# A two-layer block on one core: idle products at the opening, longer planner allowances, and modulations moved to other places

## The chip, the cores and the metric

The kernel runs on one core of one Trainium2 chip. The metric is the device time of one execution in microseconds. The kernel before took 1059.36 us as the median of three runs (1059.28 to 1059.82). The engines are named TensorE (PE in profile rows), VectorE (DVE), ScalarE (ACT), GpSimd (POOL) and SyncE (SP); SyncE's queue issues the transfers of the weights.

## The reference

Everything is fp32, for a batch of one, 512 tokens, width 1024. A first layer (a mixture of a pooling branch and of forgetting attention) feeds a second one whose norms and residuals are modulated by a vector c.

```
layer 1:  h = rmsnorm(concat(16 meta tokens, x)) * norm_g
  u, zp, q, k, v, za, f, gp, ga = split(h @ w_in)
  yp = pool(u) * silu(zp)        # 4 groups of 128 channels: trailing means over 2, 4, 8, 16, minus u
  ya = attention(q, k, v, decay from f) * silu(za)                  # 8 heads of 64
  h  = h0 + (sigmoid(gp) * (yp @ w_up_pool) + sigmoid(ga) * (ya @ w_up_attn)) @ w_out
  x  = rmsnorm(h) * final_norm_g, without the meta tokens
layer 2:  sh1, sc1, gt1, sh2, sc2, gt2 = split(silu(c) @ w_ada + b_ada)     # six modulations
  h  = rmsnorm(x) * (1 + sc1) + sh1;  q, k, v of 16 heads = h @ w_in_2
  o  = 8 stick-breaking heads, 8 heads of attention in chunks (band and bias, q and k normalised)
  x  = x + gt1 * (o @ w_o)
  h  = rmsnorm(x) * (1 + sc2) + sh2
  x  = x + gt2 * (relu(h @ w1)^2 @ w2)                              # 1024 -> 4096 -> 1024
```

## The kernel before, in words

Each fp32 operand of a large product is split into a high and a low part, and each product is done as three: high by high, high by low, low by high (`mm3`, L149). A weight arrives by one transfer into a raw tile `wr` (a ring of five), ScalarE casts it to the high part `wh`, and GpSimd or VectorE subtracts to get the low part `wl` (L128, both rings of four). Results stand in eight PSUM banks.

The stages, in the time of the profiled execution: first norm and values to about 62 us, attention and dense products of layer one to 222, the up products to 372, `w_out` and the joint norm (the final norm of layer one, and the first norm of layer two) to 424, the values and the first strip's queries and keys to 446, attention and dense products of layer two with the first rows of `w_o` to 672, the remaining rows and the second norm to 692, then the product with `w1` in a form with fewer multiplications (lines L1204 to L1206 and L1276 to L1304 write the hidden rows `hid`), from 870 on the product with `w2`.

TensorE's order is written out by the program; those of the other engines are set by a scheduler at build time. Where attention and dense products lie side by side, a planner (`weave`, L73) takes turns: each stream yields the cost of a step in ns of a planned clock, or a name to wait for, and a step that needs a result of another engine is held until an allowance (the `LAT_` constants, in planned ns) has passed since the step that makes it. The allowances are thus only numbers that set TensorE's order; nothing waits for them on the chip. In `attn2` (L1012) a unit is one strip of 128 queries of one head: `scores` (products, then softmax on the other engines), and two units later its `turn`, which transposes the weights (L1002); after eight units `pv2` multiplies by the values. `dense2` gives the queries and keys of the next pairs, of which the last four are normalised first (L861 to L885; L878 and L879 are products with the squares), and then the first rows of `w_o`.

A modulation is computed on VectorE: `ada(v, j)` (L203) loads 512 KB of `w_ada` and adds two of eight blocks of rows into an accumulator (L215 the first, L217 each other, 128x512); four steps make a half of one of the six vectors, which TensorE then sums over partitions (L234). The list `todo` holds the steps, `ada_step` takes the next, and they are sprinkled over other work. The vector 5 is the gate of the last residual.

The opening: x and `norm_g` are loaded (L292, L293), `norm_g` is spread over the partitions by TensorE (L360), VectorE normalises the first rows (L329), TensorE transposes them (L333), and ScalarE and VectorE split them (L334, L335). In the pooling branch `u_tile(g)` (L543) makes g + 1 adds of a tile with itself shifted (L555), and L558 subtracts u.

## Time and profile before

| | |
|---|---|
| median of the runs | 1059.36 us |
| profiled execution | 1057.35 us, span 1055.2 us |
| mean granted clock of TensorE | 0.994 |
| busy: TensorE, VectorE, ScalarE, GpSimd | 1012.8, 628.3, 561.8, 301.0 us |
| read from HBM | 119.82 MB, 118 GB/s over the span |

The span runs from the first to the last instruction of one execution. A row of the timeline gives start and duration, engine, line, operation, names (out<-in), tile and, in brackets, how long the engine had been idle before it and what ended that. A group of equal instructions that follow one another is one row with a count. The granted clock is a share of full speed: 1.00 is 2.4 GHz, 0.50 is 1.2 GHz.

### The profile page before, as it was taken

How to read it: one execution, taken by the hardware profiler on the slowest of the kernel's cores; microseconds unless marked ns; L12 is line 12 of the kernel's file. 1: busy time of each engine (PE TensorE's matmuls, PEld its weight loads, DVE VectorE, ACT ScalarE, POOL GpSimd, SP SyncE). 2: the span in 40 equal slices, each digit the busy share in tenths (PEclk: the TensorE clock that was granted, in tenths of full speed). 3: DMA queues.
4: the chain of work that ended last, by engine and by line, in shares of the span. 5: the costliest groups of instructions: out<-in, count | busy, mean ns of one | idle time of the engine just before them, and what ended most of it. 6: DMA issues, size and time to landing. Idle time of an engine off the chain costs nothing.

```text
span 1055.2 us, 15524 instructions
## 1 busy us (share of the span) xinstructions
PE 1012.8 (96%) x5918; PEld 857.8 (81%) x5918; DVE 628.3 (60%) x1184; ACT 561.8 (53%) x1082; POOL 301.0 (29%) x157
## 2 busy tenths in 40 slices
PE   7999999899999999999899988999999979999998
PEld 5987977768888888987678866799999978888886
DVE  6465866764533669367777476569588862611115
ACT  6365654454545645466687686347567753222220
POOL 3322123423322543203202115122121233233330
PEclk9999999999999999999999999999999999999999
DMA  8442533454543566326421234443234334633302
GB/s 238 126 122 63 154 94 102 138 138 122 149 112 100 181 198 192 128 72 189 126 63 61 68 101 140 146 113 82 66 94 120 121 120 135 177 109 100 100 20 80
DMA packets 136059, 125.54 MB, mean 119 GB/s; under 512 B 8141, under 2 KB 112417, under 8 KB 135986
## 3 DMA queue, kind: packets, MB, share of 16 engines
q1 hardware_dynamic: 135986, 124.56, 40.6%
q8 instruction: 46, 0.75, 0.3%
q14 instruction: 27, 0.22, 0.1%
HBM read 119.82 MB, written 4.73 MB: 118 GB/s over the span
## 4 chain that ended last, share of the span: by engine, by line
PE 76%; DVE 9%; issue 5%; ACT 3%; DMA 3%; POOL 3%; SPq 0%; DVEq 0%; POOLq 0%; ACTq 0%
PE ps L150 19%; PE ps L152 18%; PE ps L151 18%; PE ps L1204 4%; PE ps L1206 3%; PE ps L1205 3%; DVE ada L217 2%; PE ps L963 2%; DMA wr<-in_w_ada_dram 2%; POOL wl L128 1%; DMA wr<-in_w_in_dram 1%; PE ps L519 1%; PE ps L438 1%; PE ps L439 1%; DVE QK L427 1%
## 5 line engine op out<-in xcount | busy, mean ns | idle before, releaser
L128 POOL TENSOR_TENSOR wl<-wr,wh 128x1024 fp32r<-128x1024 f32 x99 | 248.1, 2511 | 577.7 <-ACT wh L131 567.1
L131 ACT CAST wh<-wr 128x1024 fp32r<-128x1024 f32 x130 | 136.3, 1050 | 106.5 <-PE ps L151 55.7
L150 PE MATMUL ps<-hh,wh 128*128 128x512 f32 (+1 forms) x352 | 129.7, 368 | 0.0
L151 PE MATMUL ps<-hl,wh 128*128 128x512 f32 (+1 forms) x352 | 125.1, 355 | 0.0
L152 PE MATMUL ps<-hh,wl 128*128 128x512 f32 (+1 forms) x352 | 124.8, 355 | 0.0
L150 PE MATMUL ps<-wh,T 128*128 128x512 f32 x256 | 101.0, 394 | 0.0
L152 PE MATMUL ps<-wh,T 128*128 128x512 f32 x256 | 100.4, 392 | 0.0
L151 PE MATMUL ps<-wl,T 128*128 128x512 f32 x256 | 100.2, 391 | 0.0
L217 DVE SCALAR_TENSOR_TENSOR ada<-wr,vc,ada 128x512 f32<-128x512 f32 x84 | 81.7, 972 | 11.4 <-DMA wr<-in_w_ada_dram 10.4
L150 PEld LDWEIGHTS ps<-hh,wh 128*128 128x128 f32 x352 | 66.3, 188 | 20.4 <-issue 11.5
L152 PEld LDWEIGHTS ps<-hh,wl 128*128 128x128 f32 x352 | 66.4, 189 | 9.7
L151 PEld LDWEIGHTS ps<-hl,wh 128*128 128x128 f32 x352 | 66.4, 189 | 7.7
L128 DVE TENSOR_TENSOR wl<-wr,wh 128x1024 fp32r<-128x1024 f32 x31 | 41.4, 1336 | 29.1 <-ACT wh L131 29.1
L152 PEld LDWEIGHTS ps<-wh,T 128*128 128x128 f32 x256 | 48.1, 188 | 11.4
L151 PEld LDWEIGHTS ps<-wl,T 128*128 128x128 f32 x256 | 48.1, 188 | 10.7
L150 PEld LDWEIGHTS ps<-wh,T 128*128 128x128 f32 x256 | 48.1, 188 | 10.6
L150 PE MATMUL ps<-h2h,wh 128*128 128x512 f32 (+1 forms) x144 | 54.9, 381 | 0.0
L1206 PE MATMUL ps<-QK,wl 128*128 128x256 f32 x192 | 53.7, 280 | 0.0
L1204 PE MATMUL ps<-QK,wh 128*128 128x256 f32 x192 | 53.7, 279 | 0.0
L1205 PE MATMUL ps<-PT,wh 128*128 128x256 f32 x192 | 53.4, 278 | 0.0
L152 PE MATMUL ps<-h2h,wl 128*128 128x512 f32 (+1 forms) x144 | 53.3, 370 | 0.0
L151 PE MATMUL ps<-h2l,wh 128*128 128x512 f32 (+1 forms) x144 | 53.1, 369 | 0.0
(412 smaller groups left out, 2672.6 us busy)
## 6 DMA issues: line engine op xcount, KB each, us to landing
wr<-in_w_in_dram SPq DMA_DIRECT2D x64, 512.0 KB, 5.8
wr<-in_w_dram SPq DMA_DIRECT2D x64, 512.0 KB, 4.1
wr<-in_w_ada_dram SPq DMA_DIRECT2D x48, 512.0 KB, 4.9
wr<-in_w_out_dram SPq DMA_DIRECT2D x12, 512.0 KB, 3.5
wr<-in_w_o_dram SPq DMA_DIRECT2D x12, 512.0 KB
xr<-in_x_dram SPq DMA_DIRECT2D x8, 512.0 KB
wr<-in_w_up_pool_dram SPq DMA_DIRECT2D x8, 256.0 KB
wr<-in_w_up_attn_dram SPq DMA_DIRECT2D x8, 256.0 KB, 3.3
```

The source lines that it names most:

```text
L128: (eng or pool).tensor_tensor(dst, raw, f(hi), op=OP.subtract)
L131: act.copy(dst_hi, raw)
L150: pe.matmul(ps, lh, rh, start=start, stop=False)
L151: pe.matmul(ps, lh, rl, start=False, stop=False)
L152: pe.matmul(ps, ll, rh, start=False, stop=stop)
L217: dve.scalar_tensor_tensor(acc, raw[:, q, :], cs, acc, op0=OP.mult, op1=OP.add)
L427: dve.scalar_tensor_tensor(A[e][other], src[own], scale, f(A[e][own]), op0=OP.mult, op1=OP.subtract)
L438: pe.matmul(ps, A[e][:, sa], B[e][:, sb], start=True, stop=False)
L963: pe.matmul(ps[:, d0:], ntri if j2 == j else nones, part[:, SOFF[j2]:SOFF[j2] + 512 - d0], start=False, stop=part is sl and j2 == j, skip_ ...
L1204: pe.matmul(ps, wh, bh, start=first and k == 0, stop=False, **go)
L1205: pe.matmul(ps, wh, bl, start=False, stop=False, **go)
L1206: pe.matmul(ps, wl, bh, start=False, stop=k == 3, **go)
```

## The change

`norm_g` is loaded ahead of x. Sixteen products of a constant tile with itself (`warm`, results unused) are written into TensorE's order at the opening: six at the very start, four after the spreading of `norm_g`, six ahead of the first weights product. In the last pooling group the adds are done by VectorE. Several allowances are longer, and that of a chunked unit depends on its strip. Modulation 4, which opened the list of layer two (its steps lay in the joint norm and the attention), is computed in layer one, beside the up products, three steps and not two in each of the last four of these; `ada_all()` after `weave` in layer one becomes an assertion that nothing is left. Two of the values' chunks in `v2_chunk` share banks in pairs. The steps of modulation 5 begin with a copy of a column of `hid[31]` into the accumulator, so that the accumulation stands behind the last hidden row. The diff:

```diff
@@ -34,14 +34,16 @@
 ORDER = (0, 1, 4, 2, 5, 3, 6, 7)
 LAST_SB = 3
 DENSE = (1, "v2", 4, 2, 5, 3, "v3", 6, 7)
-LAT_CA = 5600.0
+LAT_CA = 6000.0
 LAT_SM = 3200.0
 LAT_SB = 4000.0
-LAT_CM = 3200.0
+LAT_CM = (3200.0, 3800.0, 4400.0, 5000.0)
 LAT_QK = 2600.0
-LAT_SQ = 3800.0
-LAT_ADA = 4000.0
+LAT_SQ = 5000.0
+LAT_ADA = 6500.0
 LAT_PV = 600.0
+LAT_PV2 = 1500.0
+LAT_QK2 = 3800.0
 
 
 def f(ap):
@@ -146,10 +148,10 @@
         split(hi, lo, raw, eng or (dve if lo_turn[0] % dve_turn[0] == 0 else pool))
         return hi, lo
 
-    def mm3(ps, lh, ll, rh, rl, start, stop):
-        pe.matmul(ps, lh, rh, start=start, stop=False)
-        pe.matmul(ps, lh, rl, start=False, stop=False)
-        pe.matmul(ps, ll, rh, start=False, stop=stop)
+    def mm3(ps, lh, ll, rh, rl, start, stop, **go):
+        pe.matmul(ps, lh, rh, start=start, stop=False, **go)
+        pe.matmul(ps, lh, rl, start=False, stop=False, **go)
+        pe.matmul(ps, ll, rh, start=False, stop=stop, **go)
 
     def rstd(r, ss, n):
         parts = ss.shape[0]
@@ -200,7 +202,7 @@
 
     ada_acc = {}
 
-    def ada(v, j):
+    def ada(v, j, late=None):
         half, k = j // 4, 2 * (j % 4)
         raw = wts.tile([128, 2, 512], F32, name="wr", tag="wr", bufs=5)
         x = a["w_ada_2"]
@@ -208,6 +210,8 @@
                                   ap=[[6 * D, 128], [128 * 6 * D, 2], [1, 512]]))
         if k == 0:
             ada_acc[0] = consts.tile([128, 512], F32, name="ada", tag="ada", bufs=1)
+            if late is not None:
+                dve.tensor_copy(ada_acc[0][:, :1], late)
         acc = ada_acc[0]
         for q in range(2):
             cs = vc[:, V_C + k + q:V_C + k + q + 1]
@@ -289,8 +293,16 @@
 
     x_meta = wt([128, D], "PT")[:NM]
     gn = wt([1, D], "QK")
+    sp.dma_start(gn, rows(a["norm_g"], 0, 1, D, 0, D))
     sp.dma_start(xr[0], rows(a["x"], 0, 128, D, 0, D))
-    sp.dma_start(gn, rows(a["norm_g"], 0, 1, D, 0, D))
+    idle = bank()
+
+    def warm(n):
+
+        for _ in range(n):
+            pe.matmul(idle[:, :128], ones_f, ones_f, start=True, stop=True)
+
+    warm(6)
 
     wv = {}
 
@@ -358,9 +370,11 @@
     gnb = [bank(), bank()]
     for b in range(2):
         pe.matmul(gnb[b], ones_f[:1], gn[:, 512 * b:512 * b + 512], start=True, stop=True)
+    warm(4)
     load_wv(0)
     sp.dma_start(xr[1], rows(a["x"], 128, 128, D, 0, D))
     first_norm(xr[0], 128, NM, *x0)
+    warm(6)
     vt = [v_tile(t) for t in range(5)]
     next(vt[0])
     x1 = x_stats(xr[1], 128)
@@ -552,7 +566,7 @@
         prev, w = u, 1
         for q in range(g + 1):
             s = wt([128, NP], "T")
-            pool.tensor_tensor(s[:, 2 * w - 1:], prev[:, 2 * w - 1:], prev[:, w - 1:NP - w], op=OP.add)
+            (dve if g == 3 else pool).tensor_tensor(s[:, 2 * w - 1:], prev[:, 2 * w - 1:], prev[:, w - 1:NP - w], op=OP.add)
             prev, w = s, 2 * w
         pf = prev[:, NM:]
         dve.scalar_tensor_tensor(pf, pf, 1.0 / w, u[:, NM:], op0=OP.mult, op1=OP.subtract)
@@ -621,9 +635,9 @@
             ada_step()
         for m in range(8):
             yield from ups(m)
-            ada_step(2)
-
-    todo += [(v, k) for v in (0, 1, 3) for k in range(8)]
+            ada_step(2 if m < 4 else 3)
+
+    todo += [(v, k) for v in (0, 1, 3, 4) for k in range(8)]
     UT = wt([128, NP], "T")
     pool.memset(UT, 1.0)
     pool.affine_select(UT, UT, pattern=[[1, NP]], base=0, channel_multiplier=-1, compare_op=OP.is_ge, fill=0.0)
@@ -652,7 +666,7 @@
         act.copy(Cm[0:8, c0:c0 + n], src[:8, :n])
         dve.tensor_tensor(Cm[32:40, c0:c0 + n], src[:8, :n], f(Cm[0:8, c0:c0 + n]), op=OP.subtract)
     weave((SHARE1, attn1()), (1.0, dense1()))
-    ada_all()
+    assert not todo
 
     def col_norm(tts, t, hh_, hl_, gcol, bcol):
         for b in range(4):
@@ -805,7 +819,7 @@
         act.copy(V2[t][:, 256 * c:256 * c + 256], ps[:, :256])
 
     def v2_chunk(c):
-        pss = [bank() for _ in range(4)]
+        pss = [b[:, 256 * q:256 * q + 256] for b in (bank(), bank()) for q in range(2)]
         base = (1024, 1280, 2560, 2816)[c]
         for kk in range(2):
             wh, wl = weights([wcols(w_in2, 3 * D, base, 256, 4, 512 * kk)], [4, 256])
@@ -813,10 +827,11 @@
                 for q in range(4):
                     k = 4 * kk + q
                     h, l = h_of(k, 128 * t, 128)
-                    mm3(pss[t][:, :256], h, l, wh[:, q, :], wl[:, q, :], k == 0, k == KT - 1)
+                    mm3(pss[t], h, l, wh[:, q, :], wl[:, q, :], k == 0 and t % 2 == 0, k == KT - 1,
+                        skip_group_check=True)
                     yield 325
                 if kk:
-                    act.copy(V2[t][:, 256 * c:256 * c + 256], pss[t][:, :256])
+                    act.copy(V2[t][:, 256 * c:256 * c + 256], pss[t])
 
     vw = [v2_weights(0), v2_weights(1)]
     w_in2_0 = [weights([wcols(w_in2, 3 * D, c0, 128)], [KT, 128]) for c0 in (0, 512)]
@@ -859,7 +874,7 @@
         else:
             yield from gate(w_in2_tile(128 * p, q_out), p)
             yield from w_in2_tile(512 + 128 * p, k_out)
-        mark(("qk2", p))
+        mark(("qk2", p), LAT_QK2)
 
     def gate(gen, p):
 
@@ -1027,7 +1042,7 @@
                     yield ("qk2", u[0])
                 yield kind[0](*u)
                 ada_step()
-                ripe[n] = clk[0] + (LAT_SB if kind is sb else LAT_CM)
+                ripe[n] = clk[0] + (LAT_SB if kind is sb else LAT_CM[u[1]])
                 if n % 8 == 7:
                     mark(("att", u[0]), 800.0)
             if 0 <= n - LAG < len(units):
@@ -1036,7 +1051,7 @@
             m = n - LAG - 1
             if m >= 0 and m % 8 == 7:
                 p = units[m][1]
-                yield at(clk[0] + LAT_PV)
+                yield at(clk[0] + LAT_PV2)
                 yield from pv2(p, [st[p, e][2] for e in range(2)])
                 if p == LAST_SB:
                     MX[1] = wt([128, 4, 512], "Y")
@@ -1080,7 +1095,7 @@
             rows_mm(pss_o, hts[0], rows_weights(a["w_o_2"], k, kept2, ["Y", "Y", "Y", "PT"]), k, x_of, k == 0, k == KT - 1)
             yield 2560
 
-    todo += [(v, k) for v in (4, 2) for k in range(8)]
+    todo += [(v, k) for v in (2,) for k in range(8)]
     run(qk2_sb(0))
     for c in range(2):
         for t in range(2, 4):
@@ -1370,15 +1385,15 @@
     for ft in range(32):
         if ft:
             w2_operands()
+        hs, ws = held[ft]
         if 2 <= ft < 10:
-            ada(5, ft - 2)
+            ada(5, ft - 2, hid[31][:, :1])
             if ft % 4 == 1:
                 ada_due.pop()
                 gate_sum(ft // 4 - 1)
         if ft == 10:
             load_gt(5, hid[31])
             gt = gtp[5]
-        hs, ws = held[ft]
         if ft < 32 - LAST:
             for t in range(4):
                 for n in range(2):
```

Three places of the orders are shown; the changed file's lines have numbers 2 to 15 higher than those of before.

VectorE at the last pooling group, before. L483 to L490 are the softmax of a strip of the first attention, L507 and L505 copies of its transposed weights, L558 the end of the pooling group:

```order
L483 ISA T,nmx<-ps,strip,nmx 128x264
L483 ISA nmx 128x1
L489 RECIPROCAL sums<-sums 128x1
L490 TENSOR_SCALAR T<-T,sums 128x528
L507 COPY PT<-ps 128x3x128
L558 SCALAR_TENSOR_TENSOR T<-T 128x512
L128 TENSOR_TENSOR xp<-T,xp 128x512
L505 COPY PTm<-ps 16x128 x2
```

and the same place now, where L569 is the shifted add:

```order
L497 ISA T,nmx<-ps,strip,nmx 128x264
L497 ISA nmx 128x1
L569 TENSOR_TENSOR T<-T 128x527
L569 TENSOR_TENSOR T<-T 128x525
L503 RECIPROCAL sums<-sums 128x1
L569 TENSOR_TENSOR T<-T 128x521
L504 TENSOR_SCALAR T<-T,sums 128x528
L569 TENSOR_TENSOR T<-T 128x513
L521 COPY PT<-ps 128x3x128
L572 SCALAR_TENSOR_TENSOR T<-T 128x512
L519 COPY PTm<-ps 16x128
L130 TENSOR_TENSOR xp<-T,xp 128x512
```

The four adds, which stood on GpSimd, are now spread over VectorE's softmax instructions, three of them ahead of the second normalise (L490, now L504).

VectorE in the second joint norm, before; L217 is a step of a modulation, the rest belongs to the norm:

```order
L723 TENSOR_TENSOR xr<-ps,xr 128x512
L728 TENSOR_TENSOR jn_3780<-jn_3780,jn_3781 128x1
L217 SCALAR_TENSOR_TENSOR ada<-wr,vc,ada 128x512
L160 TENSOR_SCALAR rs_t<-rs_y,rs_m 128x1
L217 SCALAR_TENSOR_TENSOR ada<-wr,vc,ada 128x512
L161 SCALAR_TENSOR_TENSOR jr_3782<-rs_t,rs_y 128x1
L725 TENSOR_TENSOR xr<-xr,V 128x512
L730 TENSOR_SCALAR jn_3780<-jn_3780,jr_3782 128x1
L727 TENSOR_TENSOR jn_3817<-jn_3817,jn_3818 128x1
L217 SCALAR_TENSOR_TENSOR ada<-wr,vc,ada 128x512
```

and now:

```order
L737 TENSOR_TENSOR xr<-ps,xr 128x512
L742 TENSOR_TENSOR jn_3838<-jn_3838,jn_3839 128x1
L162 TENSOR_SCALAR rs_t<-rs_y,rs_m 128x1
L163 SCALAR_TENSOR_TENSOR jr_3840<-rs_t,rs_y 128x1
L744 TENSOR_SCALAR jn_3838<-jn_3838,jr_3840 128x1
L739 TENSOR_TENSOR xr<-xr,V 128x512
L159 TENSOR_SCALAR rs_m<-jn_3838 128x1
```

The modulation's steps are gone from between the norm's instructions.

TensorE at the end of layer-two attention, before. L1002 transposes a unit's weights, L150 to L152 with `mxs` are dense products of `w_o`'s first rows, each block four by three of them (the left-out lines repeat them):

```order
L1002 MATMUL ps<-ident,T 128x128 x2
L150 MATMUL ps<-Y,mxs 128x512
...
L152 MATMUL ps<-Y,mxs 128x512
L1002 MATMUL ps<-ident,T 128x128 x3
L150 MATMUL ps<-Y,mxs 128x512
L151 MATMUL ps<-PT,mxs 128x512
...
L151 MATMUL ps<-PT,mxs 128x512
L152 MATMUL ps<-Y,mxs 128x512
L1002 MATMUL ps<-ident,T 128x128 x4
```

and now, where L452 and L453 are the last units' scores, L1017 the transposes and L931 the products with the values:

```order
L452 MATMUL ps<-QK 128x384
L453 MATMUL ps<-lz_606,QK 128x384
L1017 MATMUL ps<-ident,T 128x128
L452 MATMUL ps<-QK 128x512
L453 MATMUL ps<-lz_606,QK 128x512
L1017 MATMUL ps<-ident,T 128x128 x9
L931 MATMUL ps<-PT,V_3933 64x512 x2
L931 MATMUL ps<-PT,V_3934 64x384 x2
L931 MATMUL ps<-PT,V_3935 64x256 x2
```

Before, a block of dense products lay ahead of each of the last two turns; now the last three turns, nine transposes in all, follow the last scores directly.

## Rows read from the trace of the kernel before

**Rows 1.** Page, part 1: busy us (share of the span), instructions.

```profile
PE 1012.8 (96%) x5918; PEld 857.8 (81%) x5918; DVE 628.3 (60%) x1184; ACT 561.8 (53%) x1082; POOL 301.0 (29%) x157
```

**Rows 2.** Waits of TensorE: releaser, us in total, times, longest.

```profile
PE ps L1204 <- DVE hid L1276: 5.4, 1, 5.4
...
PE ps L879 <- DVE PTm L128: 4.6, 4, 1.5
PE ps L1002 <- DVE sums L993: 3.5, 2, 2.3
PE ps L519 <- ACT PT L504: 3.1, 1, 3.1
PE ps L333 <- DVE PT L329: 3.1, 2, 1.8
PE ps L664 <- DVE PTm L733: 2.6, 1, 2.6
PE ps L1002 <- ACT T L992: 2.1, 2, 1.6
PE ps L878 <- ACT PTm L131: 1.9, 3, 1.0
```

**Rows 3.** Stretches: length, busy us (instructions) by engine, granted clock, DMA share, GB/s.

```profile
445.70:622.00 176.30, 167.00 (x970) 135.00 (x969) 122.52 (x251) 123.46 (x264) 34.06 (x27) 1.00 0.33 96
622.00:692.00 70.00, 64.19 (x311) 48.57 (x310) 43.05 (x113) 39.75 (x85) 21.51 (x9) 0.98 0.46 135
864.10:867.50 3.40, 3.22 (x15) 3.22 (x16) 0.46 (x2) 0.88 (x2) 0.00 (x0) 0.50 0.70 228
```

**Rows 4.** Timeline of TensorE at the start: start, duration, instruction, idle before.

```profile
4.63 3.75 PE L360 MATMUL ps<-QK,ones_f 1*128 1x512 f32 x4 [4.63 <-DMA QK<-in_norm_g_dram]
...
12.53 0.41 PE L152 MATMUL ps<-Y,hl 128*128 128x256 f32 x1
12.74 0.41 PE L150 MATMUL ps<-Y,hh 128*128 128x256 f32 x1
...
15.05 0.28 PE L152 MATMUL ps<-Y,hl 128*128 128x256 f32 x1
15.17 0.28 PE L150 MATMUL ps<-Y,hh 128*128 128x256 f32 x1
```

**Rows 5.** Timeline of GpSimd, 200 to 210 us.

```profile
203.75 2.58 POOL L128 TENSOR_TENSOR wl<-wr,wh 128x1024 fp32r<-128x1024 f32 x1
206.30 2.43 POOL L555 TENSOR_TENSOR T<-T 128x521 f32<-128x521 f32 x2
```

**Rows 6.** Timeline of VectorE, 200 to 212 us.

```profile
203.33 0.75 DVE L490 TENSOR_SCALAR T<-T,sums 128x528 f32<-128x528 f32 x1
...
208.76 0.69 DVE L558 SCALAR_TENSOR_TENSOR T<-T 128x512 f32<-128x512 f32 x1 [4.21 <-POOL T L555]
```

**Rows 7.** Timeline of all engines around 166 us.

```profile
165.94 2.38 POOL L128 TENSOR_TENSOR wl<-wr,wh 128x1024 fp32r<-128x1024 f32 x1
...
166.01 2.86 DVE L558 SCALAR_TENSOR_TENSOR T<-T 128x512 f32<-128x512 f32 x1 [0.95 <-POOL T L555]
```

**Rows 8.** Timeline of VectorE in the second joint norm.

```profile
401.82 0.62 DVE L215 TENSOR_SCALAR ada<-wr,vc 128x512 f32<-128x512 f32 x1 [1.93 <-DMA wr<-in_w_ada_dram]
...
422.27 1.00 DVE L733 TENSOR_SCALAR PTm<-xr,jr,jr 128x512 f32<-128x512 f32 x2
```

**Rows 9.** Groups of line L217, 372 to 424 us: count, min/median/max ns, starts.

```profile
L217 DVE SCALAR_TENSOR_TENSOR ada<-wr,vc,ada x7: 740/741/748, 405.9 to 418.9; 128x512 f32<-128x512 f32 x7
```

**Rows 10.** Timeline of TensorE at the end of layer-two attention.

```profile
641.80 0.52 PE L1002 MATMUL ps<-ident,T 128*128 128x128 f32 x3 [2.28 <-DVE sums L993]
```

**Rows 11.** Timeline of VectorE at the last gate's modulation.

```profile
858.74 5.15 DVE L217 SCALAR_TENSOR_TENSOR ada<-wr,vc,ada 128x512 f32<-128x512 f32 x2 [0.76 <-DMA wr<-in_w_ada_dram]
863.82 0.41 DVE L1276 TENSOR_TENSOR hid<-ps,hid 128x256 f32<-128x256 f32 x1
```

**Rows 12.** Page, part 6: loads of w_in's raw tiles, us to landing.

```profile
wr<-in_w_in_dram SPq DMA_DIRECT2D x64, 512.0 KB, 5.8
```

## The prediction

> **What bounds the kernel now.** I began with the busy table of the page: TensorE is busy for 1012.8 of 1055.2 us, 96% of the span, and it does its products one after the other [rows 1]. So the end is set by TensorE's own work, which this change leaves alone but for sixteen small products, and by whatever keeps TensorE idle or slow. Two views name that rest. The table of waits for TensorE lists single places, 1 to 5 us each [rows 2]. The stretches view gives the granted clock: from 864.1 to 867.5 us it was 0.50, the lower level (1.2 GHz), with TensorE busy 3.22 of the 3.40 us [rows 3]. There are four such stretches, each 3.4 us long, and each begins about a microsecond or less after one of the long waits of [rows 2] has ended (L519, L664, the longer L1002 by L993, L1204). Work at half rate takes twice its time, so a stretch costs 3.4 / 2 = 1.7 us: a long wait has its own length as a price and 1.7 us behind it. The opening is a fifth slow stretch: at 12.53 us products of 256 columns start 0.21 us apart, at 15.05 us 0.12 us apart [rows 4].
>
> I sum against the profiled execution, 1057.35 us long (the span of 1055.2 and 2.15 around it). The median of the runs, 1059.36, stands 2.0 above it, and I add that at the end. About 2.1 us (0.2%) is what can be told from no change here.
>
> **Opening.** TensorE waits 4.63 us for norm_g, whose load stood behind x's; the 4 pieces of L360 then take 3.75 us [rows 4]. With the two loads exchanged the pieces start about as much sooner as one issue takes, some 0.4 us, and x lands as much later: nothing net. Of the idle products six fill the wait for norm_g, four the wait for the first normalised rows (part of the 3.1 us at L333, [rows 2]), and six stand straight before the first weights product. Gain: some eleven slow products at 0.21 - 0.12 = 0.09 us, 1.0 us, if the clock is up by then, and 0.7 us since VectorE and ScalarE now do the second half of the norm ahead of a weights split. Cost: a product of 128 idle columns appears in no row. The nearest are L360's, 3.75 / 4 = 0.94 us for 512 columns at the low clock, so 0.24 us for 128. Only the last six stand in front of ready work: 1.4 us at that rate, 0.7 at twice it, which I take. Together +1.0; bounds -1.0 to +2.5 (part of the 3.1 us goes too).
>
> **Last pooling group's adds, from GpSimd to VectorE.** TensorE's L519 waits 3.1 us [rows 2]. GpSimd does a weights split of 2.58 us first and the last two adds of L555 from 206.30 [rows 5], VectorE's L558 comes at 208.76 after 4.21 us idle [rows 6], and ScalarE's copy of PT, which L519 needs, stands behind the cast of that result. The change puts four adds of about 0.7 us each (L558's price, [rows 6]) on VectorE. But in the new order three of them stand before the normalise L490, and GpSimd is free to run its split at that time. What that does is in the rows: the L558 at 166.01 us took 2.86 us where 0.69 is its price alone, and a GpSimd split ran from 165.94 for 2.38 us [rows 6, 7]. So I let one add be held until the split has ended. L490, at 203.33 before [rows 6], comes 3 to 4 us later, and TensorE, which had no wait there, waits about 2.6 us for it: most of the wait is moved, not gone. Gain 3.1 - 2.6 = 0.5, and a half chance of saving the 1.7 us behind it: +1.3. Bounds 0 (all moved) and 3.1 + 1.7 = +4.8 (no add is held).
>
> The Trainium skill, "SBUF — State Buffer", section "Who interferes with whom", speaks against this edit: VectorE shares its second pair of memory ports with GpSimd, and of two instructions that need the pair, a VectorE operation with two inputs in SBUF being one, the later is locked out until the earlier ends. The trace agrees (2.86 against 0.69 us). Without such a rule the pooling term would be its upper bound and the forecast 3.5 us lower.
>
> **One modulation moved to layer one.** In the second joint norm VectorE waits 1.93 us for a w_ada tile, spends 0.62 us on L215 [rows 8], and then 7 times 0.741 us, 5.2 us, on L217 among the norm's own instructions [rows 9]: 7.7 us in all ahead of L733 at 422.27 us [rows 8], for which TensorE's L664 waits 2.6 us [rows 2]. In the new order none of this stands there. L733 then comes up to 7.7 us earlier; it needs only 2.6. So the wait goes (2.6) and its slow stretch (1.7): +4.3. What ends last there afterwards is TensorE. Bounds +2.6 (the stretch stays) and +5 (some tenths of waiting for h2l behind the late L215 go too). The eight steps, 16 operations of 0.74 us and 8 tiles of 512 KB, now lie beside the up products of layer one, where [rows 2] has no wait of TensorE's; these products hide them, and I cost them at nothing. Without that cover VectorE's 16 operations would cost 12 us.
>
> **Allowances in layer-two attention.** From 445.7 to 622 us TensorE is busy 167.0 of 176.3: 9.3 us idle [rows 3]. The waits are L879 for PTm (4.6, four times), L878 (1.9, three times), L1002 for T (2.1, twice), and some tenths [rows 2]. The planner now puts 1.2 us more of other products ahead of L879 (LAT_SQ). Its waits are 1.15 us on average, 1.5 at most, so about 0.4 in all is left: 4.2 gained. L878 (0.63 on average) has its own allowances raised by more than that: 1.9. The allowance of a chunked strip grows by 0 to 1.8 us with its number, against 1.05 us on average at L1002: 1.3 of the 2.1. Allowances only reorder, so dense products spent early are missing later. In the new order one turn of the fifth pair has no dense product behind it. An uncovered turn of the tail waited 2.28 us [rows 10]; 0.6 of that was waited in this place anyhow, and I charge 1.7. Sum +5.7; bounds +2 (only LAT_SQ works, and the hole costs 2.2) and +8 (no hole).
>
> **Tail of the attention, 622 to 692 us.** Idle 70.0 - 64.2 = 5.8 us [rows 3], 2.28 of it at one turn [rows 10], with one slow stretch. In the new order the last nine transposes L1017 stand in a row, where before a block of twelve products lay ahead of each of the last two turns (512 columns at twice 0.12 us: 2.8 us a block). I take it that one block's cover is missed in full (2.8) while most of the 2.28 is covered now: idle about 6.6, and the stretch stays: -0.8. Bounds -3.5 (half of the second block is missed too, or a second stretch comes) and +2 (the 2.28 goes alone).
>
> **Last gate held back.** VectorE's two L217 from 858.74 us take 5.15 us in place of 1.5, as the second waits for its tile; L1276 stands behind them at 863.82 [rows 11], and TensorE's L1204 waits 5.4 us for it [rows 2]. The change begins the accumulation with a copy out of hid[31], so all of it comes after the last L1276. The wait goes (5.4) and its stretch (1.7): +7.1. Behind the held operations VectorE now has splits for the w2 products, each 24 products or 5.7 us ahead of its use, so a late tile of 3.6 us is hidden there. Bounds +5 (it is late once by 2) and +7.6.
>
> Sum: 1.0 + 1.3 + 4.3 + 5.7 - 0.8 + 7.1 = 18.6. 1057.35 - 18.6 = 1038.8, and 2.0 for the median: 1040.8 us.
>
> **Rivals.** *The attention only moves its waits.* Nothing is gained in the middle, the tail loses 3.5, the pooling adds win nothing: 1.0 + 4.3 - 3.5 + 7.1 = 8.9, so 1050.5 us. For it: the stock of dense products is fixed. Against: the waits are small and many, and their sum is 5% of that stage.
>
> *All edits land clean.* Opening 2.0, pooling 4.0, norm 4.3, middle 7, tail 1, gate 7.1: 25.4, or 1034.0 us. For it: every wait of [rows 2] above 1.7 us is met by an edit. Against: the held L558.
>
> *Slower: held tiles choke the weight ring.* All raw weights go through five buffers in SP's order. The third modulation's first tiles are issued before attention now, and up to four are held until VectorE may use them there. Meanwhile dense tiles pass through one buffer: 5.8 us of load [rows 12] and 2.6 of split [rows 5] against 5.7 of products, so each is 2.7 us late. If that lasts for the 14 tiles of the seven query and key pairs it costs 38 us against 13.7 gained elsewhere: 1083.7. It decides from 1.0 us a tile. Against: the hold should end a few microseconds into the attention, with one or two tiles passing in it.
>
> *Nothing that counts*: new gaps take the place of the old and the clock falls as often, about 1058 us.
>
> **Chances.** Forecast 0.58 (its own range 1034 to 1047), waits only moved 0.22, clean 0.10, nothing 0.05, slower 0.05. So faster 0.90, same 0.05, slower 0.05. The range for 8 in 10 runs from 1030, the clean case with the remaining upper bounds, to 1053, the moved waits with the norm's term near its lower bound.
>
> **What would show it.** Right: no wait at L1204 in the opening of the w1 products' last block, none at L664 in the second joint norm, and full clock in both places; L879's waits together under 1 us; products of 256 columns 0.12 us apart from the first. Wrong: weights splits released by a DMA after 445.7 us (the ring); more than 7 us idle in the tail. An add of L569 that takes 2 us or more beside a GpSimd split, with a new wait of 2 to 3 us in that group, shows the pooling term as forecast; none shows its upper bound. The forecast falls if the norm's and the gate's terms together give under 8 us.

## The result, and the profile after

The changed kernel takes 1045.88 us as the median of four runs (1040.94 to 1048.44), the kernel before 1059.59 in the same session: a ratio of 0.9863, with a 95% interval of 0.9822 to 0.9904. That is 13.7 us less; 18.6 were forecast. The profiled execution was the slowest of the four, 1048.44 us (span 1046.7), 8.9 us under that of before.

The page's busy row of the changed kernel, beside [rows 1]:

```profile
PE 1015.9 (97%) x5950; PEld 862.4 (82%) x5950; DVE 633.1 (60%) x1190; ACT 560.1 (54%) x1082; POOL 295.0 (28%) x153
```

TensorE is busy for 3.1 us more, the idle products among them, and the span is 8.5 us shorter. The waits of TensorE in the changed kernel, beside [rows 2] (L1017 is the L1002 of before, L515 the transpose after the normalise, L678 the L664, L452 a scores product, L834 the copy of a chunk of the values out of its bank):

```profile
PE ps L1017 <- DVE PT L1022: 3.7, 1, 3.7
PE ps L1017 <- DVE T L1009: 3.1, 3, 1.3
PE ps L452 <- DVE QK L441: 2.6, 2, 1.8
PE ps L1017 <- DVE sums L1008: 2.2, 2, 1.5
PE ps L515 <- DVE T L504: 2.2, 1, 2.2
PE ps L152 <- ACT V L834: 1.7, 3, 0.7
...
PE ps L678 <- DVE PTm L747: 0.5, 1, 0.5
```

The waits of [rows 2] for the last gate (5.4), the squares (L879 and L878, 6.5) and PT (3.1) are gone, and 0.5 us of 2.6 is left at L678. In their place stand 2.6 us for QK, 2.2 us for the normalise, 1.7 us for the copy of the values, and 9.0 us at the transposes of layer-two attention, where before had 5.6. The wait for the copy stands in all ten traces of kernels in which the values' chunks share banks (1.4 to 1.9 us) and in none of the four in which they don't.

Stretches of the changed kernel, beside [rows 3]: the slow ones, the middle and the tail of the attention, and the place of the last gate.

```profile
208.50:211.90 3.40, 3.40 (x12) 2.74 (x11) 2.36 (x6) 2.33 (x5) 0.00 (x0) 0.50 0.35 104
446.50:620.00 173.50, 165.77 (x957) 136.02 (x955) 110.36 (x239) 124.07 (x263) 38.21 (x27) 0.99 0.31 94
620.00:690.00 70.00, 60.53 (x292) 44.52 (x292) 43.35 (x110) 38.33 (x81) 22.90 (x9) 0.98 0.42 129
471.30:474.70 3.40, 3.40 (x15) 3.21 (x14) 3.40 (x8) 1.50 (x4) 0.41 (x2) 0.50 0.69 198
648.80:652.20 3.40, 3.40 (x12) 1.22 (x10) 1.46 (x7) 0.92 (x4) 0.00 (x0) 0.50 0.65 175
856.50:860.00 3.50, 3.50 (x32) 3.50 (x31) 0.42 (x1) 3.45 (x5) 3.10 (x2) 1.00 0.44 116
```

Slow stretches remain at 208.5, 471.3 and 648.8 us; at the gate's place the clock is full. The middle of the attention idles 7.7 us (9.3 before), the tail 9.5 (5.8 before).

The table splits the difference by stage. Each number is the time between the starts of two TensorE instructions that both traces have, less the same time in the trace of before; the stages are named by their ends in before. In brackets: what slow stretches cost in that stage (half of TensorE's busy time in them; under 0.5 left out), which in before is 1.7 in the stages 200 to 216, 370 to 428 and 428 to 672, and 1.6 in 858 to 868. Each row is one execution. A stage that an edit doesn't touch can differ too: gate_alone's attention is 1.1 us shorter.

```
                    to 62   200-216       370   370-428      428-672   672-858  858-868   to 1050
changed              1.4   -0.9 [1.7]    0.9   -4.6        0.7 [3.4]     0.2     -7.1       0.9
no_idle_products     0.0   -1.0 [1.7]    0.9   -4.4       -2.0 [1.7]     0.0     -7.1       0.9
ten_idle             1.5   -0.9 [1.7]    0.9   -6.1       -2.8 [1.7]     0.2     -7.1       0.9
pool_adds_back       1.3   -0.1 [1.6]    1.0   -6.1       -0.9 [3.4]     0.0     -7.1       1.0
old_allowances       1.3   -2.5          0.9   -6.1        2.4 [1.7]     0.0     -7.1       0.3
gate_alone           0.0    0.0 [1.7]    0.0    0.0 [1.7] -1.1 [1.7]     0.0     -7.1       0.0
move_alone          -0.3    1.2 [3.0]    2.0    0.0 [1.5] -7.4           0.0     -0.4 [1.4] 1.8
move_and_hold        0.0    1.2 [3.0]    1.3   -4.6       -2.4           0.0      0.0 [1.8] 0.5
no_hold              1.1   -0.9 [1.7]    1.8    7.1 [4.3] -6.2 [1.7]     0.0     -7.1       0.9
steps_later          0.5   -2.5          0.9   -6.1       -2.9 [3.2]     0.0     -7.1       1.0
split_to_vectore     0.3   -4.2          0.9   -4.4        0.3 [4.9]     0.0     -7.1       0.1
both                 1.8   -4.3          0.9   -6.1       -3.3 [3.2]     0.0     -7.1       1.0
all_in_layer_one     0.3   -4.2         18.2 [5.4] -6.1   -5.3 [3.4]     0.0     -7.1       0.1
```

(The stage 62 to 200 differs by under 0.2 us everywhere and is left out.)

### The profile page after: what moved, and what is told of

Its sections match the earlier page's. It is cut to its first block, busy times and chain, and to the rows that moved or that the text cites. A ratio compares the mean times of both kernels' runs of the same rounds, so it can differ in the third digit from the quotient of the medians.

```text
span 1046.7 us, 15606 instructions
## 1 busy us (share of the span) xinstructions
PE 1015.9 (97%) x5950; PEld 862.4 (82%) x5950; DVE 633.1 (60%) x1190; ACT 560.1 (54%) x1082; POOL 295.0 (28%) x153
## 4 chain that ended last, share of the span: by engine, by line
PE 84%; DVE 5%; issue 4%; ACT 3%; POOL 2%; DMA 2%; DVEq 0%; POOLq 0%; ACTq 0%
PE ps L152 21%; PE ps L154 20%; PE ps L153 20%; PE ps L1219 4%; PE ps L1221 4%; PE ps L1220 4%; PE ps L978 2%; PE ps L931 2%; PE ps L452 1%; PE ps L533 1%; PE ps L453 1%; DMA wr<-in_w_in_dram 1%; POOL Y L130 1%; ACT wh L133 1%; DVE ada L221 1%
## 5 line engine op out<-in xcount | busy, mean ns | idle before, releaser
L130 POOL TENSOR_TENSOR wl<-wr,wh 128x1024 fp32r<-128x1024 f32 x99 | 243.7, 2464 | 586.1 <-ACT wh L133 561.2
L152 PE MATMUL ps<-hh,wh 128*128 128x512 f32 (+1 forms) x352 | 129.8, 369 | 0.0
L152 PE MATMUL ps<-wh,T 128*128 128x512 f32 x256 | 100.8, 394 | 0.0
L221 DVE SCALAR_TENSOR_TENSOR ada<-wr,vc,ada 128x512 f32<-128x512 f32 x84 | 79.2, 943 | 7.9 <-DMA wr<-in_w_ada_dram 6.6
L152 PEld LDWEIGHTS ps<-hh,wh 128*128 128x128 f32 x352 | 66.5, 189 | 19.7 <-issue 10.8
L152 PEld LDWEIGHTS ps<-wh,T 128*128 128x128 f32 x256 | 48.1, 188 | 11.3
L152 PE MATMUL ps<-h2h,wh 128*128 128x512 f32 (+1 forms) x144 | 54.2, 377 | 0.0
L1219 PE MATMUL ps<-QK,wh 128*128 128x256 f32 x192 | 53.5, 279 | 0.0
```

Of the source, the lines that this page charges most:

```text
L130: (eng or pool).tensor_tensor(dst, raw, f(hi), op=OP.subtract)
L152: pe.matmul(ps, lh, rh, start=start, stop=False, **go)
L221: dve.scalar_tensor_tensor(acc, raw[:, q, :], cs, acc, op0=OP.mult, op1=OP.add)
L1219: pe.matmul(ps, wh, bh, start=first and k == 0, stop=False, **go)
```

## The experiments

Theory at the start: the last gate and the joint norm give what was forecast; the idle products cost instead of giving; in the attention the allowances gain what they were to gain, or only move waits, and the runs must say which.

**no_idle_products** (changed kernel)

```diff
-    idle = bank()
-    def warm(n): ...
-    warm(6)
-    warm(4)
-    warm(6)
```

> The changed kernel without its sixteen idle products; the exchanged loads stay. Theory (from the changed kernel's trace: the six products ahead of the first weights product took 2.4 us, and the clock rose at 13.9 us against 14.2 before): the idle products cost more than they give, and without them the first weights product starts near 11.4 us, the stage to 200 us ends 1 to 2 us earlier, and the time is 1 to 2 us below the changed kernel's 1045.9. Rival: they pay, and without them 11 products at the low clock come back, 1.0 us later at 200 us.

1044.17 us (1042.17 to 1049.56; ratio to before 0.9871, 0.9849 to 0.9893). The stage to 62 us takes 1.4 us less than in the changed kernel, as the theory had it, but that is one pair of executions. The five other kernels with this same opening take 0.3, 0.3, 0.5, 1.1 and 1.8 us more than before there, in the order in which their clock rose (13.9 to 17.3 us; 13.4 in this one), and the four with idle products 1.3 to 1.5. So by these ten traces the idle products cost about 0.7 us in the mean, and the opening varies less with them. The changed kernel's rows of TensorE at the start:

```profile
1.23 2.93 PE L303 MATMUL ps<-ones_f 128*128 128x128 f32 x12 [1.23 <-POOL ones_f L172]
4.09 3.78 PE L372 MATMUL ps<-QK,ones_f 1*128 1x512 f32 x4
...
11.37 2.72 PE L303 MATMUL ps<-ones_f 128*128 128x128 f32 x12
13.79 0.42 PE L152 MATMUL ps<-Y,hh 128*128 128x256 f32 x1
14.04 0.28 PE L153 MATMUL ps<-Y,hh 128*128 128x256 f32 x1
```

Twelve rows for six products: an idle product is two passes here, and the six ahead of the first weights product take 2.4 us (11.37 to 13.79), 0.2 us a pass. L372 shows the same, four rows for two products. The clock rises at 13.9 us, just as the work begins. The first six are in the way too: they last until 4.09, and without idle products the same product of `norm_g` (L364 there) starts 1.7 us sooner, at its landing:

```profile
2.43 3.75 PE L364 MATMUL ps<-QK,ones_f 1*128 1x512 f32 x4 [2.43 <-DMA QK<-in_norm_g_dram]
```

The first weights product then starts at 9.81 us (11.4 were expected), 2.1 us before that of the kernel before, and yet nothing of it is left at 62 us in this trace: TensorE waits 0.7 and 0.9 us, up to 16.5 and 17.7 us, for the cast and the split of the second half of these weights.

**ten_idle** (changed kernel)

```diff
     first_norm(xr[0], 128, NM, *x0)
-    warm(6)
```

> The changed kernel without the last six of its idle products, the ones straight ahead of the first weights product; ten stay. Theory (those six are the cost, 2.4 us on the path, and the clock gives back about 1 us): the stage to 62 us takes 1 to 1.5 us less than with sixteen, near the kernel before or up to 0.5 us under it; 1044 to 1045. Rival (the last six are what lets the clock rise): products at the low clock come back, and the stage takes the same as with sixteen.

1045.64 us (1043.75 to 1050.22; 0.9892, 0.9871 to 0.9912); the stage to 62 us as with sixteen (1.5 against 1.4). The theory fell, and the stage takes what the rival said. Its reason, that the last six let the clock rise, is not borne out: the clock rises at 14.0 us with ten and at 13.9 with sixteen. TensorE's products of the first weights in this kernel:

```profile
11.40 0.58 PE L152 MATMUL ps<-Y,hh 128*128 128x256 f32 x1
...
14.14 0.28 PE L154 MATMUL ps<-Y,hl 128*128 128x256 f32 x1
```

They begin 2.4 us earlier than with sixteen, run at half rate until 14 us, and TensorE then waits 0.7 and 0.9 us for the second half of the weights (with sixteen, 1.2). What the six cost, the low clock and these waits cost without them. In the four traces with idle products the clock rose at 12.4 to 14.0 us, in the ten others, before's among them, at 13.4 to 17.3; the products bring it forward a little and stand in the way about as much.

**pool_adds_back** (changed kernel)

```diff
-            (dve if g == 3 else pool).tensor_tensor(s[...
+            pool.tensor_tensor(s[...
```

> The changed kernel with the last pooling group's adds on GpSimd again. Theory (the wait was moved to the normalise): the wait of 3.1 us for the copy of PT returns, the wait of 2.2 us for the normalise goes, and by 216 us TensorE stands 0.5 to 1 us later than in the changed kernel. Rival (the adds on VectorE removed the wait): 3 us or more later. Second rival: the adds hinder the softmax more than they help, and TensorE stands earlier.

1046.47 us (1041.63 to 1049.32; 0.9878, 0.9858 to 0.9898). The wait for the copy of PT is 3.15 us again, the one for the normalise is gone, and 200 to 216 us takes 0.8 us more: the theory.

**split_to_vectore** (on no_idle_products)

```diff
-    ... eng or (dve if lo_turn[0] % dve_turn[0] == 0 else pool))
+    ... eng or (dve if lo_turn[0] % dve_turn[0] == 0 or lo_turn[0] == 26 else pool))
```

> The changed kernel without idle products, and with the one weights split that lies beside the pooling adds done by VectorE and not by GpSimd (nothing else runs on GpSimd then). Theory (the adds were held by GpSimd's split): each add takes 0.7 us, the wait of 2.2 us for the normalise falls under 1.2 us although VectorE has 1.2 us more to do, and the stage from 200 to 216 us takes 1 to 2.5 us less. Rival (VectorE is simply full there): the wait stays at 2 us or grows.

1042.73 us (1038.38 to 1043.72; 0.9843, 0.9823 to 0.9863). First VectorE in the changed kernel, then GpSimd's split and TensorE's wait there, each from its timeline:

```profile
203.46 3.52 DVE L569 TENSOR_TENSOR T<-T 128x527 f32<-128x527 f32 x2
...
207.01 0.70 DVE L569 TENSOR_TENSOR T<-T 128x521 f32<-128x521 f32 x1
207.63 0.49 DVE L504 TENSOR_SCALAR T<-T,sums 128x528 f32<-128x528 f32 x1
```

```profile
203.86 2.56 POOL L130 TENSOR_TENSOR wl<-wr,wh 128x1024 fp32r<-128x1024 f32 x1 [8.06 <-ACT wh L133]
```

```profile
208.27 0.92 PE L515 MATMUL ps<-ident,T 128*128 128x128 f32 x4 [2.19 <-DVE T L504]
```

Two adds took 3.52 us; alone an add takes 0.70 (207.01). The first began before GpSimd's split and took 0.70 too; the second took 2.78 and ended 0.6 us after the split had, which ran from 203.86 to 206.42. With the split on VectorE the same place reads, VectorE and then TensorE:

```profile
202.30 0.70 DVE L559 TENSOR_TENSOR T<-T 128x527 f32<-128x527 f32 x1
202.92 1.22 DVE L130 TENSOR_TENSOR wl<-wr,wh 128x1024 fp32r<-128x1024 f32 x1
...
204.12 0.69 DVE L559 TENSOR_TENSOR T<-T 128x525 f32<-128x525 f32 x1
204.73 0.49 DVE L494 TENSOR_SCALAR T<-T,sums 128x528 f32<-128x528 f32 x1
```

```profile
205.36 0.63 PE L505 MATMUL ps<-ident,T 128*128 128x128 f32 x4 [0.44 <-DVE T L494]
```

VectorE has 1.22 us more to do, every add takes 0.70, and the wait is 0.44 us in place of 2.19. One thing more differs: the third add now stands behind the normalise, which is worth one add of the difference. The stage takes 4.2 us less than before, near the upper bound of the prediction (4.8), and 3.3 less than in no_idle_products (1 to 2.5 expected), 1.7 of it a slow stretch that didn't come. So the adds were held by GpSimd's split, and VectorE's load was not the cause. The Trainium skill ("SBUF — State Buffer", "Who interferes with whom") says that of two such instructions the later is locked out until the earlier ends; both traces agree: held for 2.1 us beside the split, not at all without it.

**gate_alone** (kernel before)

```diff
+            if late is not None:
+                dve.tensor_copy(ada_acc[0][:, :1], late)
...
-            ada(5, ft - 2)
+            ada(5, ft - 2, hid[31][:, :1])
```

> The kernel before with the held-back start of the last modulation alone. Theory: the 5.4 us wait ahead of the last block of the w1 product and the slow stretch behind it go and nothing else changes: 7.1 us faster, 1052.5. Rival: what VectorE does later there comes late too, and only 3 to 4 us are gained: 1056.

1049.30 us (1047.90 to 1053.23; 0.9917, 0.9900 to 0.9934), 9.3 under the median of before. The stage 858 to 868 gives 7.1 us to the tenth, here and in every kernel that has the edit. The other 2 us are not this edit's place: 1.1 of them lie in the attention, which the edit doesn't touch. The rows of the changed kernel that answer to [rows 11], VectorE and TensorE:

```profile
855.11 0.42 DVE L1291 TENSOR_TENSOR hid<-ps,hid 128x256 f32<-128x256 f32 x1 [1.53 <-ACT hid L1290]
```

```profile
856.35 0.28 PE L1221 MATMUL ps<-QK,wl 128*128 128x256 f32 x1
856.47 0.28 PE L1219 MATMUL ps<-tsum,wh 128*128 128x256 f32 x1
```

The last add into `hid` begins at 855.11 and ends a microsecond before L1219, the product that waited for it before; TensorE goes on without a gap.

**old_allowances** (changed kernel)

```diff
-LAT_CA = 6000.0, LAT_CM = (3200.0, 3800.0, 4400.0, 5000.0), LAT_SQ = 5000.0
-LAT_PV2 = 1500.0, LAT_QK2 = 3800.0
+LAT_CA = 5600.0, LAT_CM = (3200.0,) * 4, LAT_SQ = 3800.0
+LAT_PV2 = 600.0, LAT_QK2 = 2600.0
```

> The changed kernel with the allowances in layer-two attention as before (5600; 3200 for all four strips; 3800 for the squares; 600 and 2600); the moved modulation and its allowance stay. Theory A (longer allowances only move waits): from 446 to 690 us the stage takes the same within 1.5 us, and the time is 1044 to 1048. Theory B (they gain the forecast 5 us, and something else in the stage lost as much): the stage takes 4 to 6 us longer, 1050 to 1052.

1046.47 us (1045.85 to 1047.72; 0.9885, 0.9871 to 0.9900): as the changed kernel, which looks like theory A. The stages say otherwise: 428 to 672 takes 2.4 us more than before, while in the two kernels with longer allowances and the same one slow stretch (no_idle_products, ten_idle) it takes 2.0 and 2.8 less. That is 4.3 to 5.2 us for the allowances, theory B for the stage; against the changed kernel, which has a stretch more, it is 1.7, or 3.4 with the stretches apart. The time of theory B (1050 to 1052) did not come, in part as this kernel's runs have fewer slow stretches (mean clocks 0.996 to 0.998, those of the changed kernel 0.994 to 0.997). Its waits of TensorE:

```profile
PE ps L452 <- DVE QK L441: 4.5, 2, 2.7
...
PE ps L894 <- DVE PTm L130: 1.7, 2, 1.3
```

L452 for QK is the new wait that eats part of the gain, 4.5 us here, and it stands in the changed kernel too (2.6). L894 is the squares' wait, the L879 of before. In the changed kernel, VectorE, GpSimd and TensorE in turn:

```profile
467.22 2.22 DVE L966 TENSOR_TENSOR Y<-T,Y 128x512 fp32r<-128x512 f32 x1
469.37 0.74 DVE L221 SCALAR_TENSOR_TENSOR ada<-wr,vc,ada 128x512 f32<-128x512 f32 x1
470.14 0.69 DVE L441 SCALAR_TENSOR_TENSOR QK<-ps,QK 64x512 fp32r<-64x512 f32 x1
```

```profile
466.51 2.39 POOL L130 TENSOR_TENSOR wl<-wr,wh 128x1024 fp32r<-128x1024 f32 x1 [5.03 <-DVE Y L965]
```

```profile
470.98 0.36 PE L452 MATMUL ps<-QK 128*128 128x256 f32 x1 [1.82 <-DVE QK L441]
```

VectorE's pack L441, which TensorE needs, stands behind a step of modulation 2 (L221) and behind L966, which took 2.22 us beside GpSimd's split, where 0.68 is its price alone (at 465.46).

**move_alone** (kernel before)

```diff
-            ada_step(2)
-    todo += [(v, k) for v in (0, 1, 3) for k in range(8)]
+            ada_step(2 if m < 4 else 3)
+    todo += [(v, k) for v in (0, 1, 3, 4) for k in range(8)]
...
-    todo += [(v, k) for v in (4, 2) for k in range(8)]
+    todo += [(v, k) for v in (2,) for k in range(8)]
-LAT_ADA = 4000.0
+LAT_ADA = 6500.0
```

> The kernel before with the moved modulation (its eight steps beside the up products of layer one, allowance 6500) alone. Theory (the move pays in the norm and charges elsewhere): 428 us is reached 4 to 4.5 us earlier relative to the end of the up products, the up products take 0.9 us longer (TensorE's own eight one-column products), and the attention stage from 446 to 672 us takes about 3 us longer, since the steps of the next modulation now stand in its first strips on VectorE; net 0 to 2 us faster. Rival (the loss in the attention is not the move's, but an effect of the other edits): the attention stage as before within 1 us, net 3 to 4 us faster.

1055.35 us (1053.56 to 1060.17; 0.9974, 0.9962 to 0.9985). By the medians it is 3.2 us faster than before, but the theory is wrong on both stages: the joint norm gains nothing, the attention gains much (7.4 us where 3 were to be lost). The up products take 2.0 us longer and not 0.9. TensorE's wait and VectorE's wait for a tile in the joint norm are back:

```profile
PE ps L664 <- DVE PTm L733: 3.0, 1, 3.0
```

```profile
405.00 0.58 DVE L215 TENSOR_SCALAR ada<-wr,vc 128x512 f32<-128x512 f32 x1 [2.21 <-DMA wr<-in_w_ada_dram]
```

Modulation 2 has taken the place that modulation 4 left. In the attention VectorE is freed, and the squares' waits, 6.5 us before, are 2.8 although their allowance is the old one:

```profile
PE ps L879 <- DVE PTm L128: 1.7, 2, 1.3
...
PE ps L878 <- ACT PTm L131: 1.1, 1, 1.1
```

**move_and_hold** (move_alone, and)

```diff
     weave((SHARE1, attn1()), (1.0, dense1()))
-    ada_all()
+    assert not todo
```

> The kernel before with the moved modulation, its allowance, and also the replacement of the emptying call at the end of layer one by an assertion, so that the moved modulation's last reduction stays pending and holds the next one out of the joint norm. Theory (it is this hold that frees the joint norm): L664's wait goes and 428 us is reached 4.4 us earlier against the end of the up products, where the move alone gave nothing; the attention stage takes 3 us more than before, as the held steps come in its first strips. Net about 1 to 2 us faster than before: 1056.5 to 1057.5. Rival (the norm gain needs the other edits too): the wait stays.

1054.12 us (1053.27 to 1056.30; 0.9962, 0.9949 to 0.9976). The two waits that the edit trades:

```profile
PE ps L438 <- DVE QK L427: 4.4, 2, 2.4
...
PE ps L664 <- DVE PTm L733: 0.5, 1, 0.5
```

The wait of the joint norm falls to 0.5 us and 370 to 428 takes 4.6 us less: theory. The attention gives back 5.0 of move_alone's 7.4 (neither has a slow stretch there): 4.4 us of waiting for QK appear. By these two stages the hold gains nothing on the kernel before; the medians differ by 1.2 us.

**no_hold** (on no_idle_products)

```diff
     weave((SHARE1, attn1()), (1.0, dense1()))
-    assert not todo
+    ada_all()
```

> The changed kernel without idle products and with the emptying call restored, so the last reduction is done at the end of layer one and modulation 2 may start in the joint norm. Theory: L664's wait of 2.5 to 3 us returns with its slow stretch (4.4 us lost to 428 us), and the attention stage is 2 to 4 us shorter since the two waits for QK near 465 us go: 1044.5 to 1046.5. Rival: the attention gives nothing back, 1048.5.

1047.71 us (1045.95 to 1053.57; 0.9907, 0.9886 to 0.9927), 3.5 us above no_idle_products. The joint norm's wait returns, and in the profiled execution (1053.57, the longest) at both halves of the norm, 7.7 us where 2.5 to 3 were expected (of its 7.1 us more than before, 4.3 are slow stretches):

```profile
PE ps L668 <- DVE PTm L737: 7.7, 2, 4.7
```

The attention is 4.2 us shorter, at the upper end of the theory. So the hold looks worth having here, by less than the joint norm alone shows; the intervals of the two kernels just touch.

**steps_later** (on no_idle_products)

```diff
                 yield kind[0](*u)
-                ada_step()
+                if n >= 8:
+                    ada_step()
```

> The changed kernel without idle products, and with the steps of modulation 2 begun eight units later in the second attention, where they stood before the change. Theory: the two waits for QK of 1.0 and 1.9 us near 465 to 470 us, seen without this edit, go, with the slow stretch of 1.7 us behind them; the attention stage takes 2.5 to 4.5 us less than without it: 1040 to 1041.5. Rival (the steps are not the cause; GpSimd's split and the weights ring are): the waits stay, 1044.

1043.83 us (1040.82 to 1045.46; 0.9858, 0.9839 to 0.9876). VectorE's pack now comes first, the first step of the modulation after it:

```profile
459.79 0.69 DVE L431 SCALAR_TENSOR_TENSOR QK<-ps,QK 64x512 fp32r<-64x512 f32 x1
...
461.99 0.48 DVE L219 TENSOR_SCALAR ada<-wr,vc 128x512 f32<-128x512 f32 x1
```

The waits for QK are gone. The stage takes 1.0 us less than in no_idle_products, though it has a slow stretch more (in the tail); without the stretches, 2.5 us, the lower end of what was expected. By the medians the difference is within the spread.

**both** (on no_idle_products)

```diff
+    ... or lo_turn[0] == 26 else pool))
...
+                if n >= 8:
+                    ada_step()
```

> The two edits together, on the changed kernel without idle products: the steps of modulation 2 eight units later, and the one split on VectorE. If both theories hold their gains add, since their stages lie 250 us apart: 1038 to 1040. If one fails, as that one's run alone.

1040.70 us (1039.94 to 1048.83; 0.9846, 0.9819 to 0.9873). By stages the two gains add. It has the lowest median of all and is 17.8 us under before, though its opening is the slowest (1.8); its interval overlaps the changed kernel's, so a gain over that (5 us by the medians) is likely and not shown.

**all_in_layer_one** (on split_to_vectore)

```diff
-            ada_step(2 if m < 4 else 3)
-    todo += [(v, k) for v in (0, 1, 3, 4) for k in range(8)]
+            ada_step(3 if m < 4 else 4)
+    todo += [(v, k) for v in (0, 1, 3, 4, 2) for k in range(8)]
...
-    todo += [(v, k) for v in (2,) for k in range(8)]
```

> The changed kernel without idle products, with the one split on VectorE, and with modulation 2 too beside the up products of layer one (three steps for the first four, four for the others), so that neither the joint norm nor the attention holds a step. Theory (VectorE has the time beside the up products): those take 1 us more for TensorE's eight small products, which the attention loses again; the norm stays free; the attention stage is 1 to 2 us shorter than with the later steps, 1038 to 1040. Rival (VectorE or the weights ring is full beside the up products): that stage takes 3 us or more longer, 1042 or more.

1053.18 us (1052.75 to 1054.66; 0.9952, 0.9939 to 0.9965). The rival, and far: the up products take 18 us more. SyncE's queue and TensorE near their end:

```profile
351.54 4.51 SPq L209 DMA_DIRECT2D wr<-in_w_ada_dram  x4
...
357.71 7.66 SPq L139 DMA_DIRECT2D wr<-in_w_out_dram  x2
```

```profile
362.08 0.95 PE L238 MATMUL ps<-ones_f,ada 128*128 128x1 f32 x8
367.92 0.80 PE L152 MATMUL ps<-wh,QK 128*128 128x512 f32 x1 [4.89 <-ACT wh L133]
```

Four tiles of `w_ada` were issued from 351.5 us; VectorE may use them only after TensorE's reduction L238 at 362.08, so four of the five raw buffers are held, the two tiles of `w_out` behind them take until 365.4 to be issued, and TensorE waits 4.89 us. With three more waits in this stage (0.8 and 1.7 us before, 2.2 behind it) that is 9.6 of the 18 us, and slow stretches are 5.4; what caused the two earlier waits was not followed back. This is the prediction's rival of the choked ring, one modulation further on.

## Why the prediction was right, and where it was not

The median lies in the likeliest case's own range, 5 us above the point. Two terms failed: the attention, with the held modulation put at nothing, and the opening. The others came near their size. Step by step:

*Last gate, +7.1*: 7.1, shown alone and in every combination. That the later steps stay hidden was right too: the stage behind takes 0.0 us more in gate_alone.

*Joint norm, +4.3*: 4.6 in the changed kernel, 6.1 in six other traces, in which L678 does not wait even the half microsecond (above the bound of 5). But the step named the wrong part of the change as its cause. The move alone gives nothing; the place stays free because the emptying call went, and the pending reduction then holds the next modulation out. "I cost them at nothing" failed: the moved steps cost 0.9 us beside the up products, where TensorE does eight one-column reductions more (L238), and the held ones 2.5 us (steps_later) to 5.0 (move_and_hold) in the attention's first strips. "What ends last there afterwards is TensorE" was right for that place and missed the next.

*Pooling adds, +1.3*: 0.9 with the slow stretch, 2.5 in traces without. The add held by GpSimd's split, the wait moved to the normalise (2.2 us, 2.6 forecast) and the half chance of the stretch came out as written; that the upper bound was right is shown by taking the split away (4.2).

*Opening, +1.0*: -1.4, below the lower bound. Two terms were mis-sized. One is the idle product, "0.24 us for 128". [rows 4] has four L360 instructions for two products, each of two passes; read so, a product of 128 columns costs 0.47 us at the low clock, and the six in front 2.8, not 0.7 (they took 2.4). The other is the exchange of the loads, put at "some 0.4 us": `norm_g` landed 2.2 us sooner (2.43 against 4.63), and the first six products outlasted its wait. The clock rose at 13.9 us against 14.2 before, but TensorE had spent the time up to then on the idle products.

*Attention, +5.7 and -0.8*: together -0.7 in the profiled execution, and -0.3 to +2.8 in four others with the same order there. The allowances themselves gave 4.3 to 5.2, near the 4.9 forecast, but that is luck in part. The forecast had 6.1 us from the squares (L879 and L878); the move of modulation 4 alone takes 3.7 of the 6.5 (move_alone, and old_allowances agrees), which left 2.8 for the allowances. The move's gain in the attention stood in no term, nor did two charges: the held modulation, which took most of it back, and the 1.7 us of waiting for the values' copies, with the shared banks that the prediction passed over. The tail idles 3.7 us more, just past the lower bound: the wait of 3.74 us for a copy of PT, and two of 1.2 us in the uncovered row of transposes. It idles 9.5 us, which the prediction had named as a sign of being wrong (more than 7).

In the profiled executions the last product comes 8.5 us earlier, while the medians differ by 13.7. The last gate and the joint norm give 11.7 of that, 11.4 forecast; the rest together loses 3.2 where 7.2 were to be gained. The two executions lie on opposite sides of their kernels: that of before shows a mean clock of 0.994, its runs beside the experiments 0.991 in the median, and that of the changed kernel is the slowest of four. So that the median came within the range rests in part on how often slow stretches come from one execution to the next, and in part on luck: the sum took their number from one execution. The 2.1 us that the prediction took as the least difference to be told was too small as well: the four runs spread over 7.5.

Open: the stage with the w2 products, which has no wait, takes 0.1 to 1.8 us longer in all kernels but gate_alone, from products that follow each other less closely, by one in a hundred at most. Why the tail's wait of 2.5 to 3.7 us stays in every kernel with the longer allowances wasn't tried. The shared banks, the exchanged loads and the moved modulation's allowance were not run alone, so the 1.7 us are put down to the banks by the code and by the kernels that have them.

## What to carry to other kernels

When work is moved out of a crowded place, ask what takes its place: here the next item of the same list moved up, and only a dependency that held it back kept the place free, at a price where it was let go. A term should be sized with a row whose count is set against the program's count of instructions, as one product may be two passes. And where slow stretches come and go from one execution to the next, edits are judged by stages with the stretches apart, since medians hide gains of a few microseconds; and in more than one execution, since a stage that no edit touched differed by one or two.

## What the runs showed of the hardware that was not expected

Whether a slow stretch follows a wait of about 2.2 us differs from one execution to the next with the same instructions. After the wait of 2.19 us at L515 the changed kernel ran at 0.50 for 3.4 us (its row at 208.50 above); after 2.18 us at the same line old_allowances did not:

```profile
208.20:211.60 3.40, 3.40 (x17) 2.59 (x17) 2.56 (x6) 2.13 (x4) 0.00 (x0) 1.00 0.41 122
```

Nor did steps_later after the same wait. At the waits for QK it is the same: after 1.94 us at 468.0 no_idle_products ran at 0.50 from 470.8, after 1.92 us at 467.3 ten_idle did not. The waits of 3.1 us for PT and of 5.2 to 5.4 us for `hid` came with one in every trace that has them, and in move_and_hold it was 6.8 us long at both. That is part of the spread of this kernel: its four runs show mean clocks of 0.997 at 1040.94 and 0.994 at 1048.44, where 0.003 of a span of 1046.7 are 3.1 us of lost work out of 7.5. Where the rest comes from is not shown.
